# A transformer layer on one core: the last token tile computed in halves with its mean taken off first, and five more products of ones

## The chip, the cores and the metric

The kernel runs on 1 core of a Trainium2 chip. The metric is the device time of one execution in microseconds, lower being better. It is given as the median of several executions; the profile is of one execution more.

## What is computed

One layer: windowed attention with a sink logit, then a squared-ReLU feed-forward block. The input of both is modulated by a conditioning vector, and both are followed by a residual sum with a LayerNorm. There are 256 tokens of 2048 features in f32, and the feed-forward block is 8192 wide.

```python
mod = c_act @ mod_w[i] + mod_b[i]
sh_m, sc_m, g_m, sh_f, sc_f, g_f = jnp.split(mod, 6, axis=-1)
hmix = x * (1.0 + sc_m[:, None, :]) + sh_m[:, None, :]
y = windowed_gqa_sink(hmix, ...)
x = layer_norm(DEEPNORM_ALPHA * x + (1.0 + g_m[:, None, :]) * y, ln_mix_g[i], ln_mix_b[i])
hff = x * (1.0 + sc_f[:, None, :]) + sh_f[:, None, :]
y = sq_relu_mlp(hff, mlp_w1[i], mlp_b1[i], mlp_w2[i], mlp_b2[i])
x = layer_norm(DEEPNORM_ALPHA * x + (1.0 + g_f[:, None, :]) * y, ln_mlp_g[i], ln_mlp_b[i])
```

The layer norm that counts here is the last one: `(z - mean) * rsqrt(var + eps) * g + b` over the 2048 features of each token.

## The kernel before

**Tiles and products.** The tokens lie in two tiles of 128 (t = 0 and 1), the features in four column blocks of 512 (c = 0 to 3). Weights come from memory through one queue (SP's), are split into a high part (ScalarE, ACT: wh, line 297) and a low rest (VectorE, DVE: wl, line 248), and each product is three on TensorE (PE): high by high, high by low, low by high (`mm3`, lines 553 to 555). Sums stand in PSUM banks: five under the name pa, two under pt, one under pm.

**The order.** A scheduler turns the program into one list for each engine. Around the first projection that order is written out by hand in the string STEPS: `v1` is one step of a modulation vector, `f1` one piece of the projection, `M2` the tile number 2 (the third, counted from one) of the input modulated, and `i6` six products of ones. A product of ones (`idle`, line 663) multiplies a constant by itself into a pa bank that nothing reads. `ONES_AT` gives the numbers of such products at two later places: among the last modulation products, and behind the first product of the feed-forward block.

**Modulated tile three.** `modulated(2)` has ACT make the high part (line 576) and DVE the low part (lines 577 and 578); the projection's products of that tile wait for both.

**The rows' transposes.** Between attention and the feed-forward block the normalised rows (`normed`, line 865 on ACT for the second token tile, line 867 on DVE for the first) are transposed on PE in `ff_input` (line 990), four 128 x 128 pieces for each pt bank, alternating between the token tiles.

**The end.** For the last column block (c = 3) the four pieces of each weight high and low all stay in SBUF, and the 16 feature steps run for tile 0 and then for tile 1, 48 products each. After tile 0, DVE gates and adds the block (`add_gated`, lines 836 to 838: tmp = ps x gate, z += tmp, and bn_stats), finishes the statistics, and normalises its four column blocks in two operations each (lines 1295 and 1296), a store behind each pair; this runs beside tile 1's products. For tile 1 the blocks c = 0 to 2 are scaled by -0.5 g ahead of time (`scaled`, line 1284). Behind the last product come `add_gated`, `bn_aggr` (line 1261) and `last_scalars`: the variance gives sd (ACT) and from it, in three small steps on DVE, q = -2/std, and then nmr = 0.5 x mean x q. ACT makes the diagonal matrix dg = ident x nmr (line 1309). PE holds `ident @ b` in three banks (line 1304) and adds `dg @ g` (line 1317); the last operation is then z x q + bank (line 1318). For c = 0 the bank is replaced by an operation on DVE, w (line 1313). Stores of c = 0 and 2 go through ACT's queue, c = 1 and 3 through SP's.

Of the kernel before, what the change touches and what calls it, by code (L numbers as in the profile page):

```python
# [21 lines left out]
NT = S // 128  # L22
# [6 lines left out]
LN_EPS = 1e-5  # L29
# [13 lines left out]
LOADS = ("m0 m0 w0 m1 w1 w2 x1 m1 m2 m2 m3 m4 w3 m3 w4 w5 m4 m4 w4,1 m4 x2 m5 w4,0 m5 m5 x3 m5 w4,2 x4 "  # L43
         "m6 w5,2 w5,1 m6 w5,0 m6 m6 m6 m6 m7 m6 m6 w6,1 x5 m7 m7 m7 w6,2 m7 m7 m7 w6,0 m7 w7,0 w7,1 w7,2")
STEPS = 'v1 v1 i10 M0 n4 f1 i6 f1 n5 f1 v1 p0 f1 f1 p1 f1 M1 v1 f1 f1 f1 v1 f1 v1 f1 f1 M2 v1 f1 f1 f1 f1 f1 l4 f1 l4 M3 v1 v1 p0 f1 f1 f1 v1 f1 f1 f1 v1 M4 v1'
# [14 lines left out]
def hybrid_kernel(ctx: ExitStack, tc: tile.TileContext, a, out: bass.AP):  # L60
    nc = tc.nc
    cst = ctx.enter_context(tc.tile_pool(name="cst", bufs=1))
    sml = ctx.enter_context(tc.tile_pool(name="sml", bufs=4))
# [5 lines left out]
    psa = ctx.enter_context(tc.tile_pool(name="psa", bufs=5, space=PSUM))  # L69
# [28 lines left out]
    ident = cst.tile([128, 128], F32, name="ident")  # L98
# [5 lines left out]
    eps = cst.tile([128, 1], F32, name="eps")  # L104
# [377 lines left out]
    for tok in LOADS.split():  # L482
        n = [int(v) for v in tok[1:].split(",")]
# [65 lines left out]
    def part(tiles, t, c):  # L549
        return tiles[c][:, t * 512:t * 512 + 512]  # L550

    def mm3(ps, xh, xl, wh, wl, start, stop):
        nc.tensor.matmul(ps, xh, wh, start=start, stop=False)  # L553
        nc.tensor.matmul(ps, xh, wl, start=False, stop=False)  # L554
        S.prev = nc.tensor.matmul(ps, xl, wh, start=False, stop=stop).ins  # L555
# [102 lines left out]
    def idle(n, after=None):  # L658

        if n:  # L660
            ps = psa.tile([128, 512], F32, name="pa")
        for _ in range(n):
            i = nc.tensor.matmul(ps, onesr, onesr[:, None, :].to_broadcast([128, 4, 128]), start=True, stop=True)
            if after is None:
                tc.keep_in_program_order(i)
            else:
                tc.add_manual_dep(i.ins, after.ins.name, ORDER_ONLY, reason="not sooner")
# [162 lines left out]
            nc.scalar.copy(oh, po)  # L830
            return lambda: nc.vector.tensor_sub(ol, po, f32(oh))

    def add_gated(ps, t, c, gt, stats):
        tmp = sml.tile([128, 512], F32, name="tmp", tag="t2", bufs=4)
        z = part(xs, t, c)
        nc.vector.tensor_tensor(tmp, ps, gt(c), op=OP.mult)
        nc.vector.tensor_add(z, z, tmp)
        nc.vector.bn_stats(stats[t][:, c], z)
# [144 lines left out]
    def ff_input(g):  # L983
        both, hf = [g4(F32R), g4(F32R)], g4()
        for kp in range(2):
            pt = pst.tile([128, 512], F32, name="pt")
            for i in range(2):
                k = 4 * g + 2 * kp + i
                for t in range(NT):
                    nc.tensor.transpose(pt[:, i * 256 + t * 128:i * 256 + t * 128 + 128],  # L990
                                        part(xs, t, k // 4)[:, (k % 4) * 128:(k % 4) * 128 + 128], ident)
            for i in range(2):
                k = 4 * g + 2 * kp + i
                s = slice((2 * kp + i) * 256, (2 * kp + i) * 256 + 256)
                hh, hl = (both[kp][:, i * 512 + x * 256:i * 512 + x * 256 + 256] for x in range(2))
                nc.scalar.activation(hh, pt[:, i * 256:i * 256 + 256], AF.Identity,  # L996
                                     scale=a2[:, k:k + 1], bias=b2[:, k:k + 1])
                if i:
                    nc.scalar.activation(hf[:, s], pt[:, i * 256:i * 256 + 256], AF.Identity,
                                         scale=a2[:, k:k + 1], bias=b2[:, k:k + 1])  # L1000
                else:
                    nc.vector.tensor_scalar(hf[:, s], pt[:, i * 256:i * 256 + 256], a2[:, k:k + 1],
                                            b2[:, k:k + 1], op0=OP.mult, op1=OP.add)
                nc.vector.tensor_sub(hl, hf[:, s], f32(hh))  # L1004
        return both
# [52 lines left out]
    g2 = None  # L1058
# [184 lines left out]
    st = [sml.tile([128, 4, 6], F32, name=f"st{t}", bufs=2) for t in range(NT)]  # L1243
    mid = gather(pm)
    for f in mid[:2]:
        f()
# [8 lines left out]

    ws = [S.main() for _ in range(4)]

    def last_scalars(st):

        mv = sml.tile([128, 2], F32, name="mv")  # L1260
        nc.vector.bn_aggr(mv, st)
        sd = sml.tile([128, 1], F32, name="sd")
        nc.scalar.activation(sd, mv[:, 1:2], AF.Sqrt, bias=eps)
        ve = sml.tile([128, 1], F32, name="ve")
        nc.vector.tensor_scalar_add(ve, mv[:, 1:2], LN_EPS)
        r0 = sml.tile([128, 1], F32, name="r0")
        nc.vector.reciprocal(r0, sd)
        q = sml.tile([128, 1], F32, name="qq")
        nc.vector.scalar_tensor_tensor(q, r0, ve, r0, op0=OP.mult, op1=OP.mult)
        nc.vector.scalar_tensor_tensor(q, q, -3.0, r0, op0=OP.add, op1=OP.mult)  # L1270
        nm = sml.tile([128, 1], F32, name="nmr")
        nc.vector.scalar_tensor_tensor(nm, mv[:, 0:1], 0.5, q, op0=OP.mult, op1=OP.mult)
        return q, nm

    def affine(c):
        return (gb[n][c // 2][:, (c % 2) * 512:(c % 2) * 512 + 512] for n in range(2))

    def store(t, c, z):
        q = nc.sync if c % 2 else nc.scalar
        q.dma_start(out[t * 128:t * 128 + 128, c * 512:c * 512 + 512], z)  # L1280

    def scaled(t, c):
        z, (g, b) = part(xs, t, c), affine(c)
        nc.vector.scalar_tensor_tensor(z, z, -0.5, g, op0=OP.mult, op1=OP.mult)

    for t in range(NT):
        ps = psa.tile([128, 512], F32, name="pa")
        for kg in range(4):
            ff_mm(ps, us, kg, t, ws[kg], kg == 0, kg == 3)
        if t == 0:  # L1290
            add_gated(ps, t, 3, g2, st)
            mv, rstd = norm_scalars(st[t])
            for c in (1, 0, 2, 3):
                z, (g, b) = part(xs, t, c), affine(c)
                nc.vector.scalar_tensor_tensor(z, z, mv[:, 0:1], g, op0=OP.subtract, op1=OP.mult)
                nc.vector.scalar_tensor_tensor(z, z, rstd, b, op0=OP.mult, op1=OP.add)
                store(t, c, z)
            for c in range(3):
                scaled(1, c)
    pw = {}  # L1300
    for c in (1, 2, 3):
        pw[c] = psa.tile([128, 512], F32, name="pa")
        g, b = affine(c)
        tc.keep_in_program_order(nc.tensor.matmul(pw[c], ident, b, start=True, stop=False))
    with tc.high_priority(200):
        add_gated(ps, 1, 3, g2, st)
        rstd, nm = last_scalars(st[1])
        dg = sml.tile([128, 128], F32, name="dg", tag="t2", bufs=4)
        nc.scalar.activation(dg, ident, AF.Copy, scale=nm)
    scaled(1, 3)  # L1310
    g, b = affine(0)
    w = sml.tile([128, 512], F32, name="w", tag="t2", bufs=4)
    nc.vector.scalar_tensor_tensor(w, g, nm, b, op0=OP.mult, op1=OP.add)
    for c in range(4):
        z, (g, b) = part(xs, 1, c), affine(c)
        if c:
            nc.tensor.matmul(pw[c], dg, g, start=False, stop=True)
        nc.vector.scalar_tensor_tensor(z, z, rstd, pw[c] if c else w, op0=OP.mult, op1=OP.add)
        store(1, c, z)


# [91 lines left out]
```

## Time and profile before

| | |
|---|---|
| median of 3 runs | 1071.27 us (1070.38 to 1072.18) |
| the profiled execution | 1071.01 us, span 1069.2 us |
| PE | busy 1051.6 us, 98% of the span |
| DVE | 938.8 us, 88% |
| ACT | 620.1 us, 58% |
| mean granted clock of PE | 0.999 |

A span goes from the first to the last instruction, and the execution's own time holds 1.8 us more around it. All times in the rows are counted from the span's start. Matmuls are pipelined, so a row's length holds the time to drain, and the pitch of products is read from one start to the next. An f32 product (not fp32r) shows as two records.

### The profile page before, as it was taken

The numbers are of one execution on the slowest core, as the hardware profiler recorded it, in microseconds if no ns is written. First come the engines' busy times: TensorE is split into PE (matmuls) and PEld (weight loads), VectorE is DVE, ScalarE is ACT, GpSimd is POOL, SyncE is SP. The second block draws the span as 40 slices with busy tenths as digits, with TensorE's granted clock in tenths as the row PEclk, the third lists the DMA queues.
The fourth block names the chain that finished last, engine by engine and source line by source line (L and its number), as shares of the span: only waits on it lengthen the run. The fifth ranks groups of instructions, "written<-read, shape, count | busy, mean of one in ns | idle before, by whom it ended". The sixth has DMA issues, their size and how long they took to land.

```text
span 1069.2 us, 15967 instructions
## 1 busy us (share of the span) xinstructions
PE 1051.6 (98%) x6162; PEld 853.7 (80%) x6162; DVE 938.8 (88%) x1396; ACT 620.1 (58%) x978; POOL 27.5 (3%) x54
## 2 busy tenths in 40 slices
PE   8999999999999999999999999999999999999997
PEld 6677677666677799988888888788888888888885
DVE  4689999979999998987579999999899887999997
ACT  5333347776772737643367776447677536767640
POOL 1000000001000000000000000000000001000000
PEclk9999999999999999999999999999999999999999
DMA  9999997799965998698824644974564773465742
GB/s 383 424 424 425 427 427 289 284 388 337 394 252 197 349 361 303 247 333 314 296 91 186 236 180 175 388 280 155 200 235 165 281 286 138 160 232 201 264 166 78
DMA packets 43516, 292.72 MB, mean 274 GB/s; under 512 B 5152, under 2 KB 5280, under 8 KB 9648
## 3 DMA queue, kind: packets, MB, share of 16 engines
q1 hardware_dynamic: 39456, 279.85, 68.0%
q0 software_dynamic: 3232, 10.50, 3.0%
q10 hardware_dynamic: 752, 1.35, 0.4%
q8 instruction: 48, 0.79, 0.3%
q14 instruction: 28, 0.23, 0.1%
HBM read 289.57 MB, written 2.11 MB: 273 GB/s over the span
## 4 chain that ended last, share of the span: by engine, by line
PE 87%; DMA 6%; DVE 4%; ACT 1%; issue 1%; SPq 0%; ACTq 0%; DVEq 0%
PE pa L1108 16%; PE pa L553 14%; PE pa L555 14%; PE pa L554 14%; PE pa L1110 9%; DMA raw<-in_modm 4%; PE pm L361 3%; PE pa L1081 3%; PE pa L1082 3%; PE pa L1078 3%; DVE g L401 2%; PE pa L766 1%; PE pt L810 1%; PE pa L827 1%; DMA raw<-in_w 1%; PE pt L554 1%
## 5 line engine op out<-in xcount | busy, mean ns | idle before, releaser
L297 ACT CAST wh<-raw 128x1024 fp32r<-128x1024 f32 (+1 forms) x332 | 335.9, 1021 | 268.3 <-PE pa L555 150.9
L248 DVE TENSOR_TENSOR wl<-raw,wh 128x1024 fp32r<-128x1024 f32 (+1 forms) x332 | 388.0, 1183 | 61.9 <-ACT wh L297 57.3
L553 PE MATMUL pa<-wh,g 128*128 128x512 f32 x648 | 258.1, 399 | 3.6 <-ACT g L576 2.9
L554 PE MATMUL pa<-wl,g 128*128 128x512 f32 x648 | 253.4, 391 | 0.5 <-DVE wl L248 0.5
L555 PE MATMUL pa<-wh,g 128*128 128x512 f32 x648 | 252.9, 392 | 0.9 <-DVE g L578 0.9
L1108 PE MATMUL pa<-g,wh 128*128 128x512 f32 x768 | 191.5, 391 | 0.0
L1108 PEld LDWEIGHTS pa<-g,wh 128*128 128x128 f32 x768 | 140.5, 188 | 28.4 <-issue 0.8
L553 PEld LDWEIGHTS pa<-wh,g 128*128 128x128 f32 x648 | 121.6, 188 | 40.9 <-issue 6.8
L555 PEld LDWEIGHTS pa<-wh,g 128*128 128x128 f32 x648 | 121.5, 188 | 29.7 <-DVE g L578 3.0
L554 PEld LDWEIGHTS pa<-wl,g 128*128 128x128 f32 x648 | 121.8, 188 | 25.6 <-DVE wl L248 1.2
L1110 PEld LDWEIGHTS pa<-g,wl 128*128 128x128 f32 x768 | 104.8, 190 | 7.5
L1110 PE MATMUL pa<-g,wl 128*128 128x256 f32 x768 | 107.1, 282 | 0.0
L401 DVE SCALAR_TENSOR_TENSOR g<-raw,cact,g 128x1024 f32<-128x1024 f32 x66 | 84.0, 1280 | 2.7 <-DMA raw<-in_modf 1.6
L1081 PE MATMUL pa<-g,wh 128*128 128x256 f32 x256 | 72.9, 285 | 0.2 <-DVE g L1004 0.2
L1078 PE MATMUL pa<-g,wh 128*128 128x256 f32 x256 | 72.7, 285 | 0.4 <-ACT g L996 0.3
L1082 PE MATMUL pa<-g,wl 128*128 128x256 f32 x256 | 72.3, 283 | 0.0
L248 DVE TENSOR_TENSOR raw<-raw 128x1024 fp32r<-128x1024 f32 x48 | 58.4, 1222 | 0.6 <-ACT raw L297 0.6
L297 ACT CAST raw<-raw 128x1024 fp32r<-128x1024 f32 x48 | 49.8, 1044 | 4.9 <-DVE raw L259 3.6
L401 DVE SCALAR_TENSOR_TENSOR g4b<-raw,cact,g4b 128x1024 f32<-128x1024 f32 x32 | 40.2, 1283 | 13.8 <-DMA raw<-in_modgf 13.8
L1081 PEld LDWEIGHTS pa<-g,wh 128*128 128x128 f32 x256 | 49.1, 192 | 1.4 <-DVE g L1004 0.9
L1078 PEld LDWEIGHTS pa<-g,wh 128*128 128x128 f32 x256 | 49.0, 192 | 0.8 <-ACT g L996 0.8
L1082 PEld LDWEIGHTS pa<-g,wl 128*128 128x128 f32 x256 | 49.1, 192 | 0.0
(234 smaller groups left out, 1244.1 us busy)
## 6 DMA issues: line engine op xcount, KB each, us to landing
raw<-in_w1b SPq DMA_DIRECT2D x48, 1024.0 KB, 6.6
raw<-in_w SPq DMA_DIRECT2D x40, 1024.0 KB, 7.0
raw<-in_modm SPq DMA_DIRECT2D x32, 1024.0 KB, 11.4
raw<-in_modf SPq DMA_DIRECT2D x32, 1024.0 KB, 7.3
raw<-in_wqkv SPq DMA_DIRECT2D x24, 1024.0 KB, 12.5
raw<-in_w2s SPq DMA_DIRECT2D x24, 1024.0 KB, 4.8
raw<-in_modgm SPq DMA_DIRECT2D x16, 1024.0 KB, 7.2
raw<-in_wo SPq DMA_DIRECT2D x16, 1024.0 KB, 7.3
```

What stands on the lines that cost most here:

```text
L248: self.pinned(nc.vector.tensor_sub(l[:, :w], r, f32(self.hs[n])[:, :w]))
L297: self.pinned(nc.scalar.copy(h[:, :s.shape[-1]], s))
L361: i = nc.tensor.matmul(self.ps[32 * j:32 * j + 32, :w], lhsT[j] if type(lhsT) is list else lhsT, rhs[j], start=self.first, stop=stop)
L401: nc.vector.scalar_tensor_tensor(p[:, :e], s, cact[:, kt:kt + 1], p[:, :e], op0=OP.mult, op1=OP.add)
L553: nc.tensor.matmul(ps, xh, wh, start=start, stop=False)
L554: nc.tensor.matmul(ps, xh, wl, start=False, stop=False)
L555: S.prev = nc.tensor.matmul(ps, xl, wh, start=False, stop=stop).ins
L1078: x = nc.tensor.matmul(o, wh(w, 128), hh, start=new, stop=False)
L1081: nc.tensor.matmul(o, wh(w, 128), hl, start=False, stop=False)
L1082: nc.tensor.matmul(o, wl(w, 128), hh, start=False, stop=end)
L1108: nc.tensor.matmul(ps, wh(k, 128), ff_in(k), start=k == 0, stop=False)
L1110: nc.tensor.matmul(ps[:, :256], wl(k, 128), ff_in(k)[:, :256], start=False, stop=k == NK - 1)
```

## The change

**Products of ones.** `STEPS` gets `i3` behind `M2 v1`: three products behind modulated tile three. `ONES_AT` gets a third number: two products behind the first transpose of the rows in `ff_input`.

**The last steps in halves.** For tile 1, c = 3, the feature steps 0 to 8 (`LAST = 9`) run 512 columns wide as before. Steps 9 to 15 first run for the left 256 columns in the same bank, then for the right 256 columns in a bank of their own (pr). `add_gated` takes a column slice: the left half, and the part of the right half that steps 0 to 8 left in the first bank, are gated and added with a priority that lets them run during the right half's products; the right half's seven steps follow in `add_gated(pr, ...)`. `bn_stats` runs for each half, so the statistics have a fifth slot.

**The mean first.** The banks hold `ident @ z` of the scaled blocks (c = 1, 2, 0) in the place of `ident @ b`, and a diagonal matrix dm = ident x mean x 0.5, made on DVE from the mean alone, is multiplied by g into them; the last operation is bank x q + b. For c = 3, DVE subtracts the mean and multiplies by gneg = -0.5 g (made ahead of time), then does the last operation in SBUF. nmr, dg and w go. The last four operations and their stores come in the order c = 3, 1, 2, 0, and all small steps are kept in the order of the program.

```diff
-STEPS = '... f1 f1 M2 v1 f1 f1 f1 f1 f1 l4 f1 l4 M3 ...'
+STEPS = '... f1 f1 M2 v1 i3 f1 f1 f1 f1 f1 l4 f1 l4 M3 ...'
-ONES_AT = (2, 2)
+ONES_AT = (2, 2, 2)
+LAST = 9
...
-    def add_gated(ps, t, c, gt, stats):
+    def add_gated(ps, t, c, gt, stats, cols=slice(0, 512), n=0):
         tmp = sml.tile([128, 512], F32, name="tmp", tag="t2", bufs=4)
-        z = part(xs, t, c)
-        nc.vector.tensor_tensor(tmp, ps, gt(c), op=OP.mult)
-        nc.vector.tensor_add(z, z, tmp)
-        nc.vector.bn_stats(stats[t][:, c], z)
+        z = part(xs, t, c)[:, cols]
+        nc.vector.tensor_tensor(tmp[:, cols], ps[:, cols], gt(c)[:, cols], op=OP.mult)
+        nc.vector.tensor_add(z, z, tmp[:, cols])
+        if stats:
+            nc.vector.bn_stats(stats[t][:, c + n], z)
...
-                    nc.tensor.transpose(pt[:, i * 256 + t * 128:i * 256 + t * 128 + 128],
-                                        part(xs, t, k // 4)[:, (k % 4) * 128:(k % 4) * 128 + 128], ident)
+                    x = nc.tensor.transpose(pt[:, i * 256 + t * 128:i * 256 + t * 128 + 128],
+                                            part(xs, t, k // 4)[:, (k % 4) * 128:(k % 4) * 128 + 128], ident)
+                    if (k, t) == (0, 0):
+                        idle(ONES_AT[2], x)
...
-    def last_scalars(st):
+    def last_scalars(st, g):
         mv = sml.tile([128, 2], F32, name="mv")
-        nc.vector.bn_aggr(mv, st)
+        keep(nc.vector.bn_aggr(mv, st))
+        dm = sml.tile([128, 128], F32, name="dm", tag="t2", bufs=4)
+        keep(nc.vector.tensor_scalar(dm, ident, mv[:, 0:1], 0.5, op0=OP.mult, op1=OP.mult))
...
+        z = part(xs, 1, 3)
+        keep(nc.vector.scalar_tensor_tensor(z, z, mv[:, 0:1], g, op0=OP.subtract, op1=OP.mult))
...
-        nm = sml.tile([128, 1], F32, name="nmr")
-        nc.vector.scalar_tensor_tensor(nm, mv[:, 0:1], 0.5, q, op0=OP.mult, op1=OP.mult)
-        return q, nm
+        return q, dm
...
+    gneg = sml.tile([128, 512], F32, name="w", tag="t2", bufs=4)
+    nc.vector.tensor_scalar_mul(gneg, gb[0][1][:, 512:], -0.5)
+    ps, pr = (psa.tile([128, 512], F32, name="pa") for _ in range(2))
+    left, right = slice(0, 256), slice(256, 512)
...
+    for n in range(LAST):
+        last(n, ps, slice(0, 512), n == 0, False)
+    for n in range(LAST, 16):
+        last(n, ps, left, False, n == 15)
+    with tc.high_priority(200):
+        add_gated(ps, 1, 3, g2, st, left)
+        add_gated(ps, 1, 3, g2, None, right)
+    for n in range(LAST, 16):
+        last(n, pr, right, n == LAST, n == 15)
...
-        tc.keep_in_program_order(nc.tensor.matmul(pw[c], ident, b, start=True, stop=False))
+        keep(nc.tensor.matmul(pw[c], ident, part(xs, 1, c), start=True, stop=False))
...
-        add_gated(ps, 1, 3, g2, st)
-        rstd, nm = last_scalars(st[1])
-        dg = sml.tile([128, 128], F32, name="dg", tag="t2", bufs=4)
-        nc.scalar.activation(dg, ident, AF.Copy, scale=nm)
-    scaled(1, 3)
...
+        add_gated(pr, 1, 3, g2, st, right, 1)
+        rstd, dm = last_scalars(st[1], gneg)
+    for c in (3, 1, 2, 0):
...
-            nc.tensor.matmul(pw[c], dg, g, start=False, stop=True)
-        nc.vector.scalar_tensor_tensor(z, z, rstd, pw[c] if c else w, op0=OP.mult, op1=OP.add)
+            nc.tensor.matmul(pw[c], dm, g, start=False, stop=True)
+        keep(nc.vector.scalar_tensor_tensor(z, pw.get(c, z), rstd, b, op0=OP.mult, op1=OP.add))
```

The diff adds lines, so a line of the new kernel has a number 1 to 18 higher than its counterpart. Outside the places below, the order on every engine and what each instruction waits for are the same.

PE at modulated tile three, after the change (575 and 576 are the high and low part of that tile, wh and wl the weights; 381 and 382 belong to the tile before):

```order
L556 MATMUL pa<-wh,g_382 128x512
L664 MATMUL pa<-onesr 128x512 x3
L554 MATMUL pa<-wh,g_575 128x512
L555 MATMUL pa<-wl,g_575 128x512
L556 MATMUL pa<-wh,g_576 128x512
```

The row of ones is new; the rows around it stand as before.

DVE at the end, before (g_2615 is the fourth column block of the input of the last norm, g_9671 and g_9672 are g, g_9673 and g_9674 are b, both in two pieces; r and qq are scalars):

```order
L1296 SCALAR_TENSOR_TENSOR g_2613<-g_2613,r_9923,g_9674 128x512
L1296 SCALAR_TENSOR_TENSOR g_2615<-g_2615,r_9923,g_9674 128x512
L836 TENSOR_TENSOR tmp<-pa,g4b 128x512
L837 TENSOR_TENSOR g_2615<-g_2615,tmp 128x512
L838 BN_STATS st_9680<-g_2615 128x6
L1261 BN_AGGR mv<-st_9680 128x2
L1284 SCALAR_TENSOR_TENSOR g_2615<-g_2615,g_9672 128x512
L1265 TENSOR_SCALAR ve<-mv 128x1
```

And after (g_2619 is the same fourth block, g_9681 a piece of b, w is gneg):

```order
L1302 SCALAR_TENSOR_TENSOR g_2617<-g_2617,r_9930,g_9681 128x512
L837 TENSOR_TENSOR tmp<-pa,g4b 128x256 x2
L838 TENSOR_TENSOR g_2619<-g_2619,tmp 128x256 x2
L840 BN_STATS st_9687<-g_2619 128x6
L1302 SCALAR_TENSOR_TENSOR g_2619<-g_2619,r_9930,g_9681 128x512
L837 TENSOR_TENSOR tmp<-pa,g4b 128x256
L838 TENSOR_TENSOR g_2619<-g_2619,tmp 128x256
L840 BN_STATS st_9687<-g_2619 128x6
L1267 BN_AGGR mv<-st_9687 128x2
L1269 TENSOR_SCALAR dm<-ident,mv 128x128
L1273 TENSOR_SCALAR ve<-mv 128x1
L1275 SCALAR_TENSOR_TENSOR g_2619<-g_2619,mv,w 128x512
```

Five half-wide operations now stand between the third and the fourth last step of tile 0, three behind them, and dm is made right behind the aggregation. Line 1307 (gneg) stands further up, between the first two operations of tile 0's `add_gated`.

PE at the rows' transposes, after:

```order
L992 MATMUL pt<-ident,g_2613 128x128
L664 MATMUL pa<-onesr 128x512 x2
L992 MATMUL pt<-ident,g_2613 128x128 x7
L1082 MATMUL pa<-g_3522,wh 128x256
L664 MATMUL pa<-onesr 128x512 x2
```

Before, the eight transposes followed each other; the second pair of ones was there.

More of the change, by code (lines that the diff above doesn't have):

```diff
@@ L1242, in hybrid_kernel @@
             nc.gpsimd.dma_start(gb[n][h], a["lnrow"][2 + n:3 + n, h * 1024:h * 1024 + 1024].partition_broadcast(128))
-    st = [sml.tile([128, 4, 6], F32, name=f"st{t}", bufs=2) for t in range(NT)]
+    st = [sml.tile([128, 5, 6], F32, name=f"st{t}", bufs=2) for t in range(NT)]
     mid = gather(pm)
@@ L1256, in hybrid_kernel @@
     ws = [S.main() for _ in range(4)]
-    def last_scalars(st):
+    keep = tc.keep_in_program_order
+    def last_scalars(st, g):
         mv = sml.tile([128, 2], F32, name="mv")
-        nc.vector.bn_aggr(mv, st)
+        keep(nc.vector.bn_aggr(mv, st))
+        dm = sml.tile([128, 128], F32, name="dm", tag="t2", bufs=4)
+        keep(nc.vector.tensor_scalar(dm, ident, mv[:, 0:1], 0.5, op0=OP.mult, op1=OP.mult))
         sd = sml.tile([128, 1], F32, name="sd")
-        nc.scalar.activation(sd, mv[:, 1:2], AF.Sqrt, bias=eps)
+        keep(nc.scalar.activation(sd, mv[:, 1:2], AF.Sqrt, bias=eps))
         ve = sml.tile([128, 1], F32, name="ve")
-        nc.vector.tensor_scalar_add(ve, mv[:, 1:2], LN_EPS)
+        keep(nc.vector.tensor_scalar_add(ve, mv[:, 1:2], LN_EPS))
+        z = part(xs, 1, 3)
+        keep(nc.vector.scalar_tensor_tensor(z, z, mv[:, 0:1], g, op0=OP.subtract, op1=OP.mult))
         r0 = sml.tile([128, 1], F32, name="r0")
-        nc.vector.reciprocal(r0, sd)
+        keep(nc.vector.reciprocal(r0, sd))
         q = sml.tile([128, 1], F32, name="qq")
-        nc.vector.scalar_tensor_tensor(q, r0, ve, r0, op0=OP.mult, op1=OP.mult)
-        nc.vector.scalar_tensor_tensor(q, q, -3.0, r0, op0=OP.add, op1=OP.mult)
-        nm = sml.tile([128, 1], F32, name="nmr")
-        nc.vector.scalar_tensor_tensor(nm, mv[:, 0:1], 0.5, q, op0=OP.mult, op1=OP.mult)
-        return q, nm
+        keep(nc.vector.scalar_tensor_tensor(q, r0, ve, r0, op0=OP.mult, op1=OP.mult))
+        keep(nc.vector.scalar_tensor_tensor(q, q, -3.0, r0, op0=OP.add, op1=OP.mult))
+        return q, dm
     def affine(c):
@@ L1284, in scaled @@
         nc.vector.scalar_tensor_tensor(z, z, -0.5, g, op0=OP.mult, op1=OP.mult)
[L1286 to L1299, printed above, removed]
+    ps = psa.tile([128, 512], F32, name="pa")
@@ new lines, in hybrid_kernel @@
+    for kg in range(4):
+        ff_mm(ps, us, kg, 0, ws[kg], kg == 0, kg == 3)
+    add_gated(ps, 0, 3, g2, st)
+    mv, rstd = norm_scalars(st[0][:, :4])
+    for c in (1, 0, 2, 3):
+        z, (g, b) = part(xs, 0, c), affine(c)
+        nc.vector.scalar_tensor_tensor(z, z, mv[:, 0:1], g, op0=OP.subtract, op1=OP.mult)
+        nc.vector.scalar_tensor_tensor(z, z, rstd, b, op0=OP.mult, op1=OP.add)
+        store(0, c, z)
+    for c in range(3):
+        scaled(1, c)
+    gneg = sml.tile([128, 512], F32, name="w", tag="t2", bufs=4)
@@ new lines, in hybrid_kernel, with last @@
+    nc.vector.tensor_scalar_mul(gneg, gb[0][1][:, 512:], -0.5)
+    ps, pr = (psa.tile([128, 512], F32, name="pa") for _ in range(2))
+    left, right = slice(0, 256), slice(256, 512)
+    def last(n, p, cols, start, stop):
+        s = slice((n % 2) * 256 + 128, (n % 2) * 256 + 256)
+        u, (wh, wl) = us[n // 2], ws[n // 4]
+        mm3(p[:, cols], u[:, :512][:, s], u[:, 512:][:, s], wh(n % 4)[:, cols], wl(n % 4)[:, cols], start, stop)
+    for n in range(LAST):
+        last(n, ps, slice(0, 512), n == 0, False)
@@ L1300, in hybrid_kernel @@
+    for n in range(LAST, 16):
[5 more added lines that the diff above has]
+        last(n, pr, right, n == LAST, n == 15)
     pw = {}
-    for c in (1, 2, 3):
+    for c in (1, 2, 0):
         pw[c] = psa.tile([128, 512], F32, name="pa")
-        g, b = affine(c)
-        tc.keep_in_program_order(nc.tensor.matmul(pw[c], ident, b, start=True, stop=False))
+        keep(nc.tensor.matmul(pw[c], ident, part(xs, 1, c), start=True, stop=False))
@@ L1305, in hybrid_kernel @@
     with tc.high_priority(200):
-        add_gated(ps, 1, 3, g2, st)
-        rstd, nm = last_scalars(st[1])
-        dg = sml.tile([128, 128], F32, name="dg", tag="t2", bufs=4)
-        nc.scalar.activation(dg, ident, AF.Copy, scale=nm)
-    scaled(1, 3)
[L1311 to L1314, printed above, removed]
+        add_gated(pr, 1, 3, g2, st, right, 1)
+        rstd, dm = last_scalars(st[1], gneg)
@@ L1315, in hybrid_kernel @@
+    for c in (3, 1, 2, 0):
         z, (g, b) = part(xs, 1, c), affine(c)
-        if c:
-            nc.tensor.matmul(pw[c], dg, g, start=False, stop=True)
-        nc.vector.scalar_tensor_tensor(z, z, rstd, pw[c] if c else w, op0=OP.mult, op1=OP.add)
+        if c < 3:
+            nc.tensor.matmul(pw[c], dm, g, start=False, stop=True)
+        keep(nc.vector.scalar_tensor_tensor(z, pw.get(c, z), rstd, b, op0=OP.mult, op1=OP.add))
         store(1, c, z)
```

2 lines of the change are left out of this document (1 added, 1 removed).

## The prediction

> **What bounds the kernel now.** The page comes first: busy shares, then the chain that ended last.
>
> ```profile
> PE 1051.6 (98%) x6162; PEld 853.7 (80%) x6162; DVE 938.8 (88%) x1396; ACT 620.1 (58%) x978; POOL 27.5 (3%) x54
> PE 87%; DMA 6%; DVE 4%; ACT 1%; issue 1%; SPq 0%; ACTq 0%; DVEq 0%
> ```
>
> TensorE (PE) is busy for 98% of the span. An edit helps only where PE waits, or behind PE's last dense work; an instruction added on PE costs its whole length, unless it lies in such a wait. The order of instructions outside the three edited places is the same, engine by engine, so three stretches are read.
>
> The tail is read from the timeline (start, length, engine, line, operation; idle time before it in brackets).
>
> ```profile
> 1057.29 0.39 PE L554 MATMUL pa<-g4b,g 128*128 128x512 f32 x1
> 1057.29 0.19 PEld L555 LDWEIGHTS pa<-g4b,g 128*128 128x128 f32 x1
> 1057.52 0.39 PE L555 MATMUL pa<-g4b,g 128*128 128x512 f32 x1
> ...
> 1057.75 2.73 PE L1304 MATMUL pa<-g,ident 128*128 128x512 f32 x6
> 1057.94 0.69 DVE L836 TENSOR_TENSOR tmp<-pa,g4b 128x512 f32<-128x512 f32 x1 [1.37 <-PE pa L555]
> ...
> 1059.39 0.69 DVE L838 BATCH_NORM_STATS2 st<-g 128x6 f32<-128x512 f32 x1
> ...
> 1060.12 0.26 DVE L1261 BATCH_NORM_AGGREGATE mv<-st 128x2 f32<-128x24 f32 x1
> 1060.30 0.63 DVE L1284 SCALAR_TENSOR_TENSOR g<-g,g 128x512 f32<-128x512 f32 x1
> ...
> 1060.90 0.15 DVE L1267 RECIPROCAL r<-sd 128x1 f32<-128x1 f32 x1
> ...
> 1061.55 0.16 DVE L1272 SCALAR_TENSOR_TENSOR nmr<-mv,qq 128x1 f32<-128x1 f32 x1
> 1061.74 0.40 ACT L1309 ACTIVATE dg<-ident,nmr 128x128 f32<-128x128 f32 x1 [1.02 <-DVE nmr L1272]
> 1061.74 0.75 DVE L1313 SCALAR_TENSOR_TENSOR w<-g,nmr,g 128x512 f32<-128x512 f32 x1
> 1062.19 2.84 PE L1317 MATMUL pa<-g,dg 128*128 128x512 f32 x6 [1.71 <-ACT dg L1309]
> ...
> 1063.36 2.46 DVE L1318 SCALAR_TENSOR_TENSOR g<-g,qq,pa 128x512 f32<-128x512 f32 x3
> ...
> 1064.13 2.05 SPq L1280 DMA_DIRECT2D out<-g  x2
> ```
>
> The accumulation ends near 1057.9. From there the statistics run on VectorE (DVE), then one hop to ScalarE (ACT) for dg, then three f32 products on PE. The chain view says which of them ends last:
>
> ```profile
> 1062.19 2.86 PE pa L1317 x6
> 1065.07 0.75 DVE g L1318
> ```
>
> So the end hangs on dg being late (1062.14) and on 2.86 us of products behind it, not on DVE's last additions. The last value stands at 1065.07 + 0.75 = 1065.82; the remaining 3.38 us of the 1069.2 are the last store and the end of the program, and stay.
>
> **The change, part by part.**
>
> *Products of ones, three behind modulated tile three.* The timeline there:
>
> ```profile
> 39.18 1.38 DVE L596 TENSOR_TENSOR g<-g,pa 128x512 f32<-128x512 f32 x2 [1.20 <-PE pa L555]
> ...
> 44.78 0.39 PE L555 MATMUL pa<-wh,g 128*128 128x512 f32 x1
> ...
> 46.16 0.60 ACT L576 ACTIVATE g<-g,shm,scm 128x256 fp32r<-128x256 f32 x1
> ...
> 46.81 0.50 PE L553 MATMUL pa<-wh,g 128*128 128x512 f32 x1 [1.64 <-ACT g L576]
> ```
>
> PE has nothing until ACT delivers the tile at 46.76. The ones take the bank that the second L596 addition at 39.18 has emptied by 40.56, so they start at 45.01. Products 512 wide follow each other by 0.23 us (1057.29 to 1057.52): 3 x 0.23 = 0.69, done at 45.7. Cover 1.64 us; cost 0. Without that cover they cost 0.69.
>
> *Two behind the rows' first transpose.*
>
> ```profile
> 352.79 0.44 PE L990 MATMUL pt<-ident,g 128*128 128x128 f32 x2
> 354.13 0.88 PE L990 MATMUL pt<-ident,g 128*128 128x128 f32 x6 [0.90 <-ACT g L865]
> ```
>
> The first two transposes read the first token tile; the other six wait for ACT to normalise the second. The pair of ones (0.46 us) now stands between the two, and PE has 0.90 us there: cost 0, 0.46 uncovered. What they could give is a clock that doesn't fall; the windows view (busy time of PE, PEld, DVE, ACT and POOL, then clock, DMA share and GB/s) shows none to save in this execution:
>
> ```profile
> 46.00:48.00 2.00, 1.01 (x3) 0.58 (x4) 1.37 (x3) 0.76 (x2) 0.00 (x0) 1.00 1.02 426
> 352.00:354.00 2.00, 1.20 (x18) 0.40 (x10) 2.00 (x8) 1.69 (x3) 0.00 (x0) 1.00 0.92 348
> 1058.00:1069.00 11.00, 5.32 (x12) 1.81 (x10) 7.24 (x15) 0.69 (x2) 0.00 (x0) 0.93 0.27 103
> ```
>
> Clock 1.00 at both places; it falls only in the tail. The Trainium skill (TensorE: Matmul & The Clock Gate, Part 1) has the clock halved after an idle window of about 3.4 us; by that rule too, gaps of 1.64 and 0.90 us leave nothing to save. Value taken: 0 for both.
>
> *The halves on PE.* 27 products stay 512 wide; 21 become 42 that are 256 wide. Such products stand in the first feed-forward block:
>
> ```profile
> 359.13 0.28 PE L1082 MATMUL pa<-g,wl 128*128 128x256 f32 x1
> ...
> 360.80 0.28 PE L1081 MATMUL pa<-g,wh 128*128 128x256 f32 x1
> ```
>
> 14 steps in 1.67 us: 0.119 each, with a fresh weight load per product. 42 x 0.119 = 5.00 against 21 x 0.227 = 4.77: PE ends 0.23 later, near 1058.15, and the left half is complete at 1058.15 - 2.50 = 1055.65.
>
> *DVE ahead of the right half.* The first token tile's last operations share DVE with the left half:
>
> ```profile
> 1048.20 0.69 DVE L836 TENSOR_TENSOR tmp<-pa,g4b 128x512 f32<-128x512 f32 x1 [0.61 <-PE pa L555]
> 1048.92 0.69 DVE L837 TENSOR_TENSOR g<-g,tmp 128x512 f32<-128x512 f32 x1
> ...
> 1053.83 2.74 DVE L1296 SCALAR_TENSOR_TENSOR g<-g,r,g 128x512 f32<-128x512 f32 x4
> L867 DVE TENSOR_SCALAR g<-g,mv,r 128x512 f32<-128x512 f32 x4 | 2.0, 542 | 0.0
> L1035 DVE TENSOR_TENSOR rl<-rl 128x256 f32<-128x256 f32 x48 | 20.2, 420 | 0.0
> 357.05 0.76 DVE L1004 TENSOR_TENSOR g<-g,g 128x256 fp32r<-128x256 f32 x2
> ```
>
> Before, four L1296 steps were done at 1056.57 and DVE idled 1.37 us. Now the new scaling of g by -0.5 stands between the first two operations. By L867 it takes 0.54, of which 0.07 overlaps: the second starts at 49.29 instead of 48.92, and all behind it 0.37 later. The bounds are 0.1 (it fits the pause between dependents) and 0.54. Three of the four L1296 steps, by 2.74/4 = 0.67 each, end at 1053.83 + 0.37 + 2.03 = 1056.2; the left half has been waiting since 1055.65. Five half-wide operations that don't wait for their neighbour follow each other by 0.76 - 0.42 = 0.34: 1.70, to 1057.9. Then the fourth L1296 step, 0.67, to 1058.6. The right half of the product, ready at 1058.15, so waits 0.45 us for DVE. This is the price of the order in which the rows stand.
>
> *From the right half to the mean.* Three half-wide dependent operations: a 512-wide one steps 0.72 (1057.94 to 1059.39 in two), 0.03 over its length, so a half takes 0.42 + 0.03 = 0.45: 1.35, to 1059.93. The aggregation steps 0.29: 1060.22, against about 1060.40 before. Only 0.18 is gained so far.
>
> *From the mean to the end.* dm is made on DVE from the mean alone. The nearest rows, 128 columns lying between them:
>
> ```profile
> L577 DVE TENSOR_SCALAR g<-g,scm,shm 128x256 f32<-128x256 f32 x16 | 6.5, 408 | 1.7 <-ACT g L576 1.7
> L155 DVE TENSOR_SCALAR sc<-sc 128x192 f32<-128x192 f32 x1 | 0.3, 261 | 0.2 <-ACT sc L153 0.2
> ```
>
> I take 0.25: dm stands at 60.47, where dg stood at 1062.14. PE's f32 products with the identity, 2.57 us in six passes of 0.43, now start at 1058.0 to 58.15 and free PE at 60.5 to 60.7, so the products with dm run from about 60.6 to 63.45. DVE: ve, then the subtraction of the mean from the last quarter (0.75 long, 0.67 step), from 60.48 to the reciprocal at 61.15; from there to the first last-stage operation 0.65, as from 1060.90 to 1061.55 before: 61.80. Four of these by 0.67 and the last 0.75 long: 61.80 + 2.01 + 0.75 = 64.56. nmr, w and dg are gone. The products (63.45) are done before the last operation asks for its bank (63.81): PE is covered by 0.36 us, and if this cover goes, its excess is added. The store that ends last moves from SP's queue to ACT's; each issues one 256 KB store just before it, 0.67 instead of 0.85 us ahead. I take no cost.
>
> Sum: 65.82 - 64.56 = 1.26 us earlier. Bounds: 1.26 + 0.45 = 1.7 if nothing held DVE, and 0.8 if the last stage, reading PSUM, steps 0.82 (2.46/3, set by PE there) instead of 0.67. The profiled execution took 1071.01 us, 0.26 under the median of 1071.27: 1071.01 - 1.26 = 1069.75, and at the median 1070.0. That is 0.12%, inside the 0.2% (2.1 us) that a measurement of this kernel can tell from no change.
>
> **The rivals.**
>
> *The clock did fall in the timed runs.* The three runs spread by 1.8 us (1070.38 to 1072.18), and one fall costs about that: the tail shows the clock can be halved after thin PE work, and half speed over a stretch like 352.8 to 356.2 costs up to 1.7 us. If the median run had one such fall and the ones prevent it: 1071.27 - 1.26 - 1.7 = 1068.3. Against it: the clock of 1.00 above. It decides if timed runs of before exceed the profiled one for this reason. Chance 0.13.
>
> *The halves are bound by weight loads.* Each half needs its own load, and a load takes 0.19 us (row 1057.29) where the half's product streams in 0.12. If loads didn't overlap: 42 x 0.19 = 7.98 against 4.77, PE ends at 1061.13, DVE has long been free, and the end is 64.56 + (61.13 - 58.58) = 67.11: 1.29 us slower, 1072.6. It decides from a step at which PE ends at 58.58 + 1.26 = 1059.84, 1.92 later than before: (4.77 + 1.92)/42 = 0.159 us. Against it speak the 0.119 of rows 359.13 and 360.80, of the same shapes. The Trainium skill (TensorE: Matmul & The Clock Gate, Part 3, What overlaps and what doesn't) has loads overlap running products only in other row groups; the rows here contradict that. Chance 0.04.
>
> *The ones or the halves do nothing.* If the left half gave no lead, because DVE is late by another 0.8 us, or the five ones fell on the path (0.69 + 0.46 = 1.15), 1071.2 to 1071.4. The rows' order and the two gaps speak against it. Chance 0.08.
>
> **How the numbers follow.** Forecast 0.75, rivals 0.13, 0.04 and 0.08. Around the forecast a median of three moves by about 0.5 (an estimate from the 1.8 us between the lowest and the highest run of before) and the bounds by -0.5 to +0.5. The range 1068.7 to 1071.4 leaves out the larger part of the clock rival and the slower one. Faster by over 0.2% means under 1069.13: most of the clock rival and a small part of the forecast, 0.15. Slower means over 1073.41: the weight-load rival with noise or a second mishap, 0.05. Within: 0.80.
>
> **What would show it.** The profile after should have the span near 1067.9; ones inside the gaps at 45 and 353, the next products where they were; the 256-wide steps of 0.12; DVE without idle time from the left half until the mean; L1336's last operation ending 1.2 us before the old 1065.82, with DVE and no longer PE ending last in the chain. A step over 0.16 for the halves, PE last in the chain, or a fall of the clock ahead of the tail would make the prediction wrong.

## The result, and the profile after

The changed kernel takes 1074.72 us (median of 8 runs, 1073.91 to 1076.14) against 1071.56 us for the kernel before on the same chip: a ratio of 1.0027, 95% interval 1.0018 to 1.0037. It is 3.2 us slower; 1070.0 and a range up to 1071.4 were forecast.

The page of the changed kernel: busy time of PE, and the shares of the chain that ended last. (Lines of the code stand 1 to 18 further on than before.)

```profile
PE 1055.0 (98%) x6188; PEld 856.2 (80%) x6188; DVE 939.5 (88%) x1401; ACT 619.9 (58%) x977; POOL 27.5 (3%) x54
PE 83%; DMA 8%; DVE 7%; ACT 1%; issue 1%; SPq 0%; DVEq 0%; ACTq 0%
```

PE's share of the chain fell from 87 to 83% and DVE's rose from 4 to 7%. Most of that lies far ahead of the tail, as 3% of the span are 32 us. That the end now hangs on DVE, as forecast, is seen in the last pieces of the chain, where PE's last piece starts at 1052.90 and DVE's follow from 1053.16 on:

```profile
1052.90 0.24 PE pa L556
...
1053.16 0.69 DVE tmp L837
...
1066.58 2.07 DVE g L1336 x3
```

Waiting for loads (DMA) rose from 6 to 8% of the chain, which no step of the forecast speaks of.

**The tail came out as written.** The timeline of the changed kernel's end:

```profile
1062.66 0.73 DVE L1302 SCALAR_TENSOR_TENSOR g<-g,r,g 128x512 f32<-128x512 f32 x1
...
1062.86 0.28 PE L556 MATMUL pa<-g4b,g 128*128 128x256 f32 x1
1062.98 2.74 PE L1328 MATMUL pa<-g,ident 128*128 128x512 f32 x6
1063.32 0.42 DVE L837 TENSOR_TENSOR tmp<-pa,g4b 128x256 f32<-128x256 f32 x1
...
1064.69 0.29 DVE L1267 BATCH_NORM_AGGREGATE mv<-st 128x2 f32<-128x30 f32 x1
...
1065.01 0.28 DVE L1269 TENSOR_SCALAR dm<-ident,mv 128x128 f32<-128x128 f32 x1
...
1065.28 0.74 DVE L1275 SCALAR_TENSOR_TENSOR g<-g,mv,w 128x512 f32<-128x512 f32 x1
1065.55 2.74 PE L1335 MATMUL pa<-g,dm 128*128 128x512 f32 x6
1065.94 0.15 DVE L1277 RECIPROCAL r<-sd 128x1 f32<-128x1 f32 x1
...
1066.58 0.75 DVE L1336 SCALAR_TENSOR_TENSOR g<-g,qq,g 128x512 f32<-128x512 f32 x1
1067.24 2.06 DVE L1336 SCALAR_TENSOR_TENSOR g<-pa,qq,g 128x512 f32<-128x512 f32 x3
```

From the start of the identity's products to the last value it is 1062.98 to 1069.30, 6.32 us, where it was 1057.75 to 1065.82, 8.07. Of these 1.75 us the halves take back 0.27 on PE, and the end of the program 0.22 (1069.30 to 1072.9 is 3.60, before 3.38). Net gain: 1.26 us.

**But PE reached this tail 5.23 us late** (1062.98 against 1057.75), 0.27 by the halves and 4.96 by something ahead of them. Two waits for loads, from the timeline of before, and then of after:

```profile
72.81 0.75 DVE L399 TENSOR_SCALAR g<-raw,cact 128x1024 f32<-128x1024 f32 x1 [0.21 <-DMA raw<-in_modm]
74.22 0.74 PE L555 MATMUL pa<-wh,g 128*128 128x512 f32 x2 [0.19 <-DVE g L578]
...
279.46 1.28 DVE L401 SCALAR_TENSOR_TENSOR g<-raw,cact,g 128x1024 f32<-128x1024 f32 x1 [1.45 <-DMA raw<-in_modf]
```

```profile
74.06 0.75 DVE L400 TENSOR_SCALAR g<-raw,cact 128x1024 f32<-128x1024 f32 x1 [1.31 <-DMA raw<-in_modm]
75.46 0.73 PE L556 MATMUL pa<-wh,g 128*128 128x512 f32 x2 [1.28 <-DVE g L579]
...
282.12 1.28 DVE L402 SCALAR_TENSOR_TENSOR g<-raw,cact,g 128x1024 f32<-128x1024 f32 x1 [2.54 <-DMA raw<-in_modf]
```

Each wait is 1.1 us longer. Around the first, the loads themselves run slower; the windows view from 60 to 120 us, before and then after (the last figure is GB/s), where the DMA engines are busy all the time in both:

```profile
60.00:120.00 60.00, 57.52 (x442) 42.23 (x436) 56.58 (x84) 19.16 (x25) 1.91 (x2) 1.00 1.01 425
```

```profile
60.00:120.00 60.00, 55.95 (x437) 41.22 (x436) 55.16 (x80) 19.33 (x25) 1.91 (x2) 1.00 1.01 419
```

In this stretch PE goes from 0.18 to 1.60 us late, by the starts of the same products in both traces. The second wait is another matter. It is as long in e4, a kernel of the experiments below in which every tile lies where it lay before and loads run at 426 GB/s:

```profile
280.81 1.28 DVE L401 SCALAR_TENSOR_TENSOR g<-raw,cact,g 128x1024 f32<-128x1024 f32 x1 [2.68 <-DMA raw<-in_modf]
```

So the 1.1 us that PE loses behind it are not shown to come from the addresses; why this wait varies is open. By the rows' transposes PE is 2.55 us late (354.13 before, 356.68 after). The rest, to 4.96, builds up slowly while PE never waits long. The first of nine products in a row and the feed-forward product behind the nine, and one product near the end; before, then after:

```profile
606.77 0.39 PE L553 MATMUL pa<-wh,sc 128*128 128x512 f32 x1
...
608.81 0.39 PE L1108 MATMUL pa<-g,wh 128*128 128x512 f32 x1
...
1008.24 0.39 PE L555 MATMUL pa<-raw,sc 128*128 128x512 f32 x1
```

```profile
356.68 0.77 PE L992 MATMUL pt<-ident,g 128*128 128x128 f32 x5 [0.28 <-ACT g L867]
...
609.61 0.40 PE L554 MATMUL pa<-wh,sc 128*128 128x512 f32 x1
...
611.71 0.40 PE L1112 MATMUL pa<-g,wh 128*128 128x512 f32 x1
...
1013.19 0.39 PE L556 MATMUL pa<-raw,sc 128*128 128x512 f32 x1
```

Nine products took 2.04 us and now take 2.10: 233 ns from start to start, not 227. Nothing was added there, and on every engine the instructions and their order are those of before. What differs is where the tiles lie. The statistics tile went from four to five pieces, 96 to 120 bytes a partition; with its four buffers padded to 128, every tile allocated behind it (tmp, raw, wh, wl, g4, g4b) lies 128 bytes further on in SBUF, while `sc` and `ident` ahead of it stay. In the kernel before, raw, wh, wl, g4 and sc all begin at multiples of 256 bytes.

### The profile page after: what moved, and what is told of

It reads as the page before. It is cut to its first block, busy times and chain, and to the rows that moved or that the text cites. A ratio compares the mean times of both kernels' runs of the same rounds, so it can differ in the third digit from the quotient of the medians.

```text
span 1072.9 us, 16023 instructions
## 1 busy us (share of the span) xinstructions
PE 1055.0 (98%) x6188; PEld 856.2 (80%) x6188; DVE 939.5 (88%) x1401; ACT 619.9 (58%) x977; POOL 27.5 (3%) x54
## 4 chain that ended last, share of the span: by engine, by line
PE 83%; DMA 8%; DVE 7%; ACT 1%; issue 1%; SPq 0%; DVEq 0%; ACTq 0%
PE pa L1112 16%; PE pa L554 13%; PE pa L556 13%; PE pa L555 13%; PE pa L1114 8%; DMA raw<-in_modm 4%; PE pa L1085 3%; PE pm L362 3%; PE pa L1086 3%; PE pa L1082 3%; DMA raw<-in_w 2%; DVE g L402 2%; DVE wl L249 1%; PE pa L767 1%; DMA raw<-in_wqkv 1%; DMA raw<-in_modf 1%
```

## The experiments

### Undoing one part of the change

The first four runs share a kernel before of 1072.09 us. Theory: the moved addresses cost the time, and the rest of the change gains what was forecast. Rival: the edits themselves, products of ones or halves, cost it.

**e1_moved**: the kernel before, with nothing but the larger statistics tile.

```diff
-    st = [sml.tile([128, 4, 6], F32, name=f"st{t}", bufs=2) for t in range(NT)]
+    st = [sml.tile([128, 5, 6], F32, name=f"st{t}", bufs=2)[:, :4] for t in range(NT)]
```

> The kernel before with one edit: the statistics of the last norm get room for five slots and use four, so that every tile that lies behind them in SBUF moves up by 128 bytes, as in the changed kernel. No instruction is added or moved. Theory 1 (addresses): the tiles' new places cost the 4.4 us that the changed kernel lost outside its tail (3.2 slower in all, and 1.2 to 1.3 us gained in the tail by the profile), so about 1076. Theory 2 (the five products of ones, or the longer list of instructions, cost it): 1071.5, as before.

Measured: 1075.66 us, ratio 1.0031 (1.0021 to 1.0042), 420 GB/s. One digit, with no instruction changed, costs 3.3 us (2.3 to 4.5); the 4.4 us that the theory has to explain lie at the upper end of this.

**e2_restored**: the changed kernel, with the statistics in the spare table `kk` of the rotary embedding, so that all other tiles lie as before.

```diff
-        return trig
+        return trig, kk
...
-                trig = rotary_tables()
+                trig, spent = rotary_tables()
...
-    st = [sml.tile([128, 5, 6], F32, name=f"st{t}", bufs=2) for t in range(NT)]
+    st = [spent[:, t, :30].rearrange("p (c s) -> p c s", s=6) for t in range(NT)]
```

> The changed kernel whole, but with the last norm's statistics kept in a table that is no longer needed by then, so that every other tile lies where it lay in the kernel before. Same instructions in the same order. Theory 1 (addresses): 1071.56 - 1.26 = 1070.3. Theory 2 (ones or instructions): 1074.7, as the changed kernel.

Measured: 1069.99 us, ratio 0.9986 (0.9977 to 0.9995), 426 GB/s. It beats both kernels; by the ratio it is 1.5 us (0.5 to 2.5) faster than the kernel before, where 1.26 was forecast. That the median falls on the forecast's 1070.0 is in part luck, as the kernel before took 1072.09 here and not 1071.27. Its timeline at the end:

```profile
1057.67 2.74 PE L1328 MATMUL pa<-g,ident 128*128 128x512 f32 x6
...
1058.01 0.41 DVE L837 TENSOR_TENSOR tmp<-pa,g4b 128x256 f32<-128x256 f32 x1
...
1061.27 0.75 DVE L1336 SCALAR_TENSOR_TENSOR g<-g,qq,g 128x512 f32<-128x512 f32 x1
1061.93 2.06 DVE L1336 SCALAR_TENSOR_TENSOR g<-pa,qq,g 128x512 f32<-128x512 f32 x3
```

PE arrives at 1057.67 (before the change 1057.75), and the last value stands at 1063.99 instead of 1065.82.

**e3_no_ones**: the changed kernel without `i3` and with `ONES_AT = (2, 2, 0)`. **e4_ones_only**: the kernel before with the five ones and nothing else.

> The changed kernel without its five new products of ones. Theory 1 (addresses): 1074.7, unchanged, since the tiles still lie 128 bytes higher. Theory 2 (ones): about 1070.3, the tail's gain alone.

> The kernel before with the five new products of ones and nothing else; all tiles lie as before. Theory 1 (addresses): 1071.5, as the ones lie in gaps of 1.64 and 0.90 us. Theory 2 (ones): about 1076.

Measured: 1074.09, ratio 1.0024 (1.0015 to 1.0032), and 1071.95, ratio 0.9995 (0.9985 to 1.0005). Neither taking the ones away nor adding them moves the time by what this measurement can tell. They lie in the gaps as forecast; the changed kernel's timeline:

```profile
45.19 0.85 PE L664 MATMUL pa<-onesr 128*128 128x512 f32 x3
46.99 0.50 PE L554 MATMUL pa<-wh,g 128*128 128x512 f32 x1 [0.94 <-ACT g L577]
...
355.57 0.72 PE L664 MATMUL pa<-onesr 128*128 128x512 f32 x2
```

### Which address, and which distance

Ten more kernels, unused tiles aside, are the kernel before (q2: the changed kernel), with groups of tiles moved. The pad is one line ahead of a pool:

```diff
+    pada = ctx.enter_context(tc.tile_pool(name="pada", bufs=1)).tile([128, 32], F32, name="pada")
     raws = ctx.enter_context(tc.tile_pool(name="raws", bufs=RAWS))
```

p1 has it ahead of the pool of wh; p2 ahead of raw and of wh; p3 twice as large ahead of raw; q3 ahead of raw; q4 ahead of g4; r1 ahead of raw and g4; r2 ahead of raw, wh and the early raw buffers. p4 puts `cst.tile([128, 32], F32, name="pada")` ahead of all tiles. q1 is e1 with a pad ahead of raw. q2 is

```diff
-    st = [sml.tile([128, 5, 6], F32, name=f"st{t}", bufs=2) for t in range(NT)]
+    st = [sml.tile([128, 6, 6], F32, name=f"st{t}", bufs=2) for t in range(NT)]
...
-        rstd, dm = last_scalars(st[1], gneg)
+        rstd, dm = last_scalars(st[1][:, :5], gneg)
```

> The kernel before with an unused tile of 128 bytes a partition between the buffers of raw and those of wh: wh, wl, g4 and g4b stand 128 bytes further on, raw and everything ahead of it where it was. Theory A (loads into places that are no multiple of 256 bytes land more slowly; some 2.5 of the 4.4 us of e1): the five raw buffers are unmoved, only the few early loads that go into g4b are, so under 1 us of that remains, and the rate from 60 to 120 us is near 425 GB/s. Theory B (the matmuls lose about 2 us because their two operands, wh or raw against sc, stand at another distance): products of wh with sc are slow (236 ns instead of 227), products of raw with sc as before (229). Time by A and B together: about 1073 to 1074, ratio 1.001 to 1.002. If instead every moved tile matters alike, 1075.5 as e1.

> The kernel before with raw 128 bytes further on and wh, wl, g4, g4b 256 bytes further on. Theory A (128-byte places of raw slow the loads): rate from 60 to 120 us near 419 GB/s, +2.5 us. Theory B (distance of the matmul's operands): raw with sc slow (233), wh with sc as before if 256 bytes are a period (227), or changed again if they are not. Time about 1075, ratio 1.002 to 1.003. A rival, that g4 and g4b at 128-byte places cost the time rather than raw: 1072.1, no change.

> The kernel before with raw, wh, wl, g4 and g4b all 256 bytes further on. If what matters is being a multiple of 256 bytes: no change, 1072.1, 425 GB/s, pitches of 227 and 229 ns. If it is a multiple of 512 or more (raw now starts at a multiple of 2048): a change of either sign, up to 3 us, and the rate from 60 to 120 us tells whether it is the loads.

> The kernel before with 128 unused bytes ahead of all tiles, so that every tile, sc and the identity too, stands 128 bytes further on and all distances are as before. Theory B says that the matmuls' pitches stay at 227 and 229 ns, so only the loads' part of e1 is lost: about 1074, ratio 1.002. If the absolute place sets the pitch too: as e1, 1075.5, with 236 and 233 ns. If neither place but only the distance matters, for the loads too: 1072.

> The kernel before with the ring of temporaries (tmp) and the small tiles behind it 128 bytes further on, raw, wh, wl, g4 and g4b 256. So far the load rate from 60 to 120 us was 419 to 420 GB/s in the four kernels where tmp had moved by 128 and 424 to 426 in the others, wherever raw stood. Theory D (the place of the temporaries sets the load rate): 419 to 420 GB/s, pitches as before (227 to 229 ns); the loads' part alone, about 1073.5, ratio 1.0014 as with every tile moved. Rival E (128 bytes of raw against the tiles ahead of sc, or all moved tiles together): 425 GB/s, 1072.2, no change.

> The changed kernel with the statistics of the last normalisation in tiles of six pieces instead of five, of which one is not used: every tile behind them then stands 256 bytes further on than in the kernel before instead of 128. If 256 bytes are the period for loads and products alike, the loss of the changed kernel is gone and the tail's gain stays: 1070.3, ratio 0.9985, 425 GB/s, 228 ns. If the temporaries' place matters at more than 256 bytes: 1072 to 1074.7.

> The kernel before with raw, wh, wl, g4 and g4b 128 bytes further on and the temporaries where they were. Theory D: 425 GB/s, pitches slow (236 for wh with sc, 233 for raw with sc); only the products' part is lost, 1074.0, ratio 1.0018. Rival E: 420 GB/s and 1075.5, as when the temporaries move too.

> The kernel before with g4 and g4b alone 128 bytes further on. If the pitch hangs on the two tiles that a product reads and weights are loaded from, wh, wl and raw with sc stay at 227 to 229 ns, and only products that mix g4 with wh can change (230 instead of 228.8): at most 0.8 us, 1072.0 to 1072.9. If g4's place, written while the others are read, slows wh and raw with sc as well: 1073.5 or more.

> The kernel before with the five raw buffers, wh and wl 128 bytes further on, and g4, g4b and the three early raw buffers 256. Theory F (the loads are slower only when all eight buffers that they land in stand 128 off): 424 to 425 GB/s from 60 to 120 us. Theory G (slower when raw and the wh and wl that are split out of it stand 128 off together): 419 to 420 GB/s. The products: wh with g4 now differ by 128, so these pitches go from 227 to 232 ns as in q4, wh with sc to 236, and the time to 1080 or more.

> The kernel before with all eight raw buffers (and g4b) at 128 off, wh, wl and g4 256 further on. Theory F: 419 to 420 GB/s from 60 to 120 us. Theory G: 424 to 425 GB/s. The products: raw with sc 233 ns, wh with sc and wh with g4 as before (227 to 228 ns); about 1076.

The table gives the shift in bytes of each group against the kernel before (g4b and the three early raw buffers share a place and move as g4; in r2 they move by 384), the load rate from 60 to 120 us, and the mean time in ns from one 512-wide product to the next between 500 and 1040 us, worked out from the records of each trace (steps over 260 ns left out), for products that stream wh against weights from sc and from g4. The kernel before took 1072.04 us in the median beside the four p kernels, 1072.23 beside the q and 1072.5 beside the r kernels.

| kernel | tmp | raw | wh, wl | g4 | GB/s | wh, sc | wh, g | us | ratio (95%) |
|---|---|---|---|---|---|---|---|---|---|
| before | 0 | 0 | 0 | 0 | 425 | 227.5 | 227.3 |  | |
| after | 128 | 128 | 128 | 128 | 419 | 235.7 | 227.8 | 1074.72 | 1.0027 (1.0018 to 1.0037) |
| e1 | 128 | 128 | 128 | 128 | 420 | 235.9 | 227.6 | 1075.66 | 1.0031 (1.0021 to 1.0042) |
| e2 | 0 | 0 | 0 | 0 | 426 | 227.3 | 227.4 | 1069.99 | 0.9986 (0.9977 to 0.9995) |
| p1 | 0 | 0 | 128 | 128 | 425 | 235.5 | 227.8 | 1073.93 | 1.0016 (1.0007 to 1.0024) |
| p2 | 0 | 128 | 256 | 256 | 424 | 228.2 | 228.0 | 1074.79 | 1.0027 (1.0017 to 1.0036) |
| p3 | 0 | 256 | 256 | 256 | 425 | 227.6 | 227.4 | 1072.82 | 1.0005 (0.9996 to 1.0014) |
| p4 (sc too) | 128 | 128 | 128 | 128 | 419 | 228.6 | 227.5 | 1073.59 | 1.0014 (1.0005 to 1.0024) |
| q1 | 128 | 256 | 256 | 256 | 425 | 227.5 | 227.4 | 1072.14 | 0.9999 (0.9991 to 1.0008) |
| q2 | 256 | 256 | 256 | 256 | 425 | 228.0 | 227.5 | 1071.35 | 0.9989 (0.9979 to 0.9998) |
| q3 | 0 | 128 | 128 | 128 | 419 | 235.2 | 227.9 | 1076.48 | 1.0040 (1.0028 to 1.0052) |
| q4 | 0 | 0 | 0 | 128 | 425 | 227.9 | 232.0 | 1080.32 | 1.0076 (1.0064 to 1.0088) |
| r1 | 0 | 128 | 128 | 256 | 424 | 235.9 | 232.2 | 1082.29 | 1.0087 (1.0058 to 1.0116) |
| r2 | 0 | 128 | 256 | 256 | 421 | 227.4 | 227.7 | 1074.77 | 1.0024 (1.0012 to 1.0036) |

**The products** follow, for the most part, the distance of the two tiles that they read. wh with sc is slow in every row where the two differ by 128, and only there; 256 leave it as it was (p2, p3, q1, q2), and so does moving sc along (p4). wh with g4, fast in all rows where both move together, turns slow when the two differ by 128 (q4, r1). That is the larger price, as most products are of this kind: 7.6 and 8.7 parts in a thousand (in r1 the products with sc are slow as well). q4's expectation missed this: it allowed 0.8 us and 8 were lost. The timelines of before, and then of q4, over the same 76 products:

```profile
683.04 0.39 PE L553 MATMUL pa<-wh,g 128*128 128x512 f32 x1
...
700.27 0.39 PE L554 MATMUL pa<-wl,g 128*128 128x512 f32 x1
```

```profile
688.72 0.39 PE L554 MATMUL pa<-wh,g 128*128 128x512 f32 x1
...
706.46 0.39 PE L555 MATMUL pa<-wl,g 128*128 128x512 f32 x1
```

17.23 us became 17.74: 226.7 to 233.4 ns each. And the nine products of above in p4, where all distances are kept:

```profile
610.52 0.39 PE L554 MATMUL pa<-wh,sc 128*128 128x512 f32 x1
...
612.56 1.98 PE L1109 MATMUL pa<-g,wh 128*128 128x512 f32 x8
```

2.04 us, as before. Products of raw with sc go from 228.9 to 232.6 ns in p2 and in r2, where raw is 128 off. Two things don't fit. These products are slow in p1 too (231.8), where neither of the two has moved. And the feed-forward products that stream g4 against weights from wh, some 670 in this stretch, go from 229.1 ns to 230.4 in p2 and r2, where both tiles still begin at multiples of 256 and only raw (in r2 g4b with it), which these products don't read, is 128 off (p3, p4, q1 and q2: 229.0 to 229.1). In p2 some 130 of them are 4 ns or more longer and most of the others are as before; it adds up to 0.9 us. So the distance of a product's own two tiles is not all of it. Which reads meet, and whether the tiles of a neighbouring product, of another engine or of a load count too, stays open.

**The loads** depend on where raw itself lies, not on a distance: p4 is as slow as e1 (419 and 420 GB/s). p2's expectation missed here: with five raw buffers moved, 419 was expected and 424 measured. Theory D of q1, that the temporaries' place does it, fell (q1: 425; q3: 419 without it). So did theory G of r1 (424). Theory F stands in part: 419 to 421 GB/s in all six kernels of which all eight raw buffers were seen at 128 (after, e1, e3, p4, q3, r2), 424 or more where only three or five were (p1, q4, p2, r1). Why five of eight cost so little is open. The Trainium skill (DMA: Bandwidth & Descriptors, How a descriptor splits into AXI transactions) cuts a transfer into pieces of 256 bytes that begin at multiples of 256, told there for what is read; here it is the place written that moved. By it a row of 8192 bytes that lands 128 off needs 33 pieces for 32, 3% more (an estimate); the period of 256 agrees with p3 and q2, and the loss measured is 1.4%.

**The two parts together.** By the ratios, p4 prices slow loads alone at 1.5 us (0.5 to 2.6), and p1 slow products with loads as before at 1.7 (0.8 to 2.6). Their sum, 3.2, is what e1 lost with both (3.3).

**q2** shows the simplest cure: with six pieces instead of five, 128 bytes more, all lies 256 further on, and the loss is gone: 1071.35 us against 1072.23, a ratio whose interval overlaps that of e2.

## Why the prediction was wrong, by its own steps

- **The failed step** is the sentence in its first part that the order of instructions outside the three places is the same, "so three stretches are read". The order was the same; the durations were not. The statistics' fifth slot was in the diff, and its place in SBUF was never priced. It cost 4.4 us (1.0027 against 0.9986 of 1071), more than three times the whole forecast gain. In the profiled execution PE is 2.55 us late by 354 us and loses 2.4 more after it. Of the former, 1.4 come with the slower loads from 60 to 120 us; the 1.1 behind the second wait are not shown to be the addresses' work, as e4 loses 1.5 there with no tile moved. Of the latter, some 2.0 are longer products; 0.45 are a single step near 680 us that q2 shows too, at 256 bytes.
- **The tail** was right: 1.26 forecast, 1.26 in the profile after, and 1.15 in e2's (8.07 to 6.32 us, less 0.27 for the halves and 0.33 behind the last value). That it came out to the hundredth is luck, as two of its terms were off and made up for each other: the right half waited 0.2 us for DVE, not 0.45 (1062.86 + 0.28 to 1063.32 in the tail of after), and the end behind the last value took 0.2 to 0.3 more, where no cost was taken. In the working, 2.74/4 is 0.685 and not 0.67; about 0.67 is the step from one start to the next, (2.74 - 0.75)/3 = 0.66, so the sum stands.
- **Halves bound by weight loads**: not so. The pitch of the 256-wide products is 0.12 (1062.86 to 1062.98), as taken, and PE paid 0.27 for 0.23.
- **The ones** cost nothing that shows, as taken. That they had nothing to save was wrong. The profiled execution of before had a clock of 1.00 at both places; others did not. The windows view (clock, DMA share and GB/s last) of e3 and of p3, neither with ones, and of e4 with them:

```profile
48.00:50.00 2.00, 2.00 (x7) 1.58 (x7) 1.38 (x2) 0.00 (x0) 0.00 (x0) 0.65 1.04 434
50.00:52.00 2.00, 2.00 (x12) 1.13 (x15) 1.00 (x2) 0.32 (x1) 0.00 (x0) 0.50 1.00 408
```

```profile
358.00:362.00 4.00, 4.00 (x17) 3.59 (x18) 2.53 (x11) 4.00 (x9) 0.00 (x0) 0.50 1.01 426
```

```profile
48.00:50.00 2.00, 2.00 (x10) 1.39 (x8) 1.90 (x3) 0.00 (x0) 0.00 (x0) 1.00 1.01 426
50.00:52.00 2.00, 2.00 (x37) 1.60 (x37) 1.99 (x3) 1.05 (x1) 0.00 (x0) 1.00 1.03 424
358.00:362.00 4.00, 3.90 (x29) 3.30 (x28) 2.58 (x11) 4.00 (x8) 0.00 (x0) 1.00 1.02 428
```

  The clock fell to half behind exactly the two gaps that the ones fill. So the argument that gaps of 1.64 and 0.90 us are too short to cost any clock failed too. With ones, the mean clock was 0.999 or more in 41 of 42 executions of four kernels; without, it was 0.998 or less in 44 of 96 executions of before. These took 1072.8 us in the median, the other 52 took 1071.4. So the clock rival's mechanism was real, at 1.4 us in nearly half of the executions, 0.6 on average. e4 alone doesn't show that in time: its interval of 0.1% to each side of 0.9995 holds such a gain and none.

## What to carry to other kernels

A tile that grows by a few bytes moves every tile behind it: compare the addresses of two versions, not only the order of their instructions, and pad so that large tiles keep their places modulo 256 bytes. When all instructions of an unchanged stretch are slightly slower, measure pitch and load rate there, and rebuild the kernel before with nothing but the addresses changed. One profiled execution doesn't show what happens in half of the others; look at the granted clock of all of them.

## What the runs showed of the hardware that was not expected

The time from one product to the next depends on where tiles lie in SBUF, above all on the distance of the two that it reads: 227 to 228 ns, and 232 to 236 where it is off by 128 bytes; for wh with sc followed by wl with sc, 227.8 and 238.4 (before and e1, from the records of 24 pairs). A smaller rise, from 229.1 to 230.4 ns, met products whose own tiles had kept their places modulo 256 (g4 with wh in p2 and r2). The Trainium skill (SBUF — State Buffer, A bandwidth-pool intuition that's wrong) gives the weight loads a read port of their own beside that of the moving tile. By that alone the distance should not matter; here it does, and the measurement decides. Loads into buffers that all lie 128 bytes off multiples of 256 ran at 419 to 421 GB/s instead of 425.
